# The opening of a two-layer encoder trunk in another order: gate sums split from their rows, weight splits cut in two, second tokens turned between products

## The chip, the cores and the metric

One core of one Trainium2 chip runs the whole program. The metric is the device time of one execution in microseconds (us). Each time below is either a median over runs or comes from one execution that the hardware profiler recorded.

## The reference, cut to what matters

The program computes a trunk of two layers over 1024 tokens of width 1024. What the change touches is the very first part of layer 0: the modulation of the first norm, that norm, and the first columns of the input projection.

```python
cond = jax.nn.silu(c)
for l in range(DEPTH):
    mod = cond @ w_mod[l] + b_mod[l]
    sh_a, sc_a, gt_a, sh_f, sc_f, gt_f = [m[:, None, :] for m in split_cols(mod, (D,) * 6)]
    h = rms_norm(x, g_attn[l]) * (1 + sc_a) + sh_a
    proj = h @ w_in[l]
    ...                      # three head groups, output projection, SwiGLU, residuals
return rms_norm(x, g_final)
```

Everything is fp32. A product of two fp32 matrices is made of three matmuls on operands that are split into a high part and a low rest (high by high, low by high, high by low).

## The kernel before, in words

**Engines and order.** In the opening the instruction streams of TensorE (PE), ScalarE (ACT), VectorE (DVE) and the load queue (SP) are pinned: each engine runs its instructions in the order in which the source issues them. GpSimd (POOL) is not pinned there. SP is a queue too: a load that must wait for a buffer, or for one of eight load semaphores that go round, holds up all loads behind it. So the text of the source between `wc_stage` and the end of the opening is the schedule, and nothing else decides it.

**What the opening computes.** The first 2048 columns of `w_mod` (shift and scale of the first norm) are needed before any token can be normed. They are cut into four *pairs* p = 0..3; a pair gives shift and scale for two of the eight blocks of 128 channels. Each pair is loaded in two halves, i = 2p and 2p+1, of 1 MB each (`gm_load(i)`, two transfers of 512 KB, a ring of three buffers). A half holds four groups of 128 rows. Three of them are multiplied by the condition and added up on DVE (`mod_add`, tile `ga`), the fourth is a one-row matmul on PE (`ps_mod<-gm`, called a *row* here). When both halves are in, a second matmul adds the DVE sum to the row (`ps_mod<-ga`, the *sum*), ACT copies it out (`gr`), PE turns it into columns (`ps_m`, the *turn*), and DVE makes `mod` and `gsc` of it (`gemv_finish`).

**Norm and products.** `h_blocks(half, rows, ns)` norms two blocks for 512 tokens: on DVE `nt` twice, on ACT `hh` twice (high part), on DVE `hl` twice (low part). `c_first(n)` then multiplies block n of the first 512 tokens with the weights of the third head group, into four banks: 12 matmuls. These weights come in four loads (`wc_stage`), each split into `whi` (ACT) and `wlo` (DVE) by `w_split`.

**The second tokens.** x is loaded token by token (`xn`), squared on ACT (`x_square`), turned by PE with a copy by ACT (`x_turn`, tile `xt`; `ps_x`), and its row factors are spread over the partitions by PE (`spread`, `ps_r`). For tokens 512 to 1023 this happens at the end of the opening, then `h_blocks(1, ...)` norms all eight blocks, and the projection of these tokens (`c_proj(4, 5)`, 48 matmuls, still `ps_c`) follows. `turn_vecs(1, v1)` is a small transpose for layer 1 (`pst`), with a DVE copy (`vecs`). `c_norm_first` norms the keys and queries of the first 128 tokens and hands them to POOL for the rotation.

**Behind the opening** comes a loop over t = 0..9 in which DVE and POOL norm and rotate one token block after another, PE projects and turns (`pq`, `pk`), and two more weight blocks (`wab`) are split. The first of these splits is the first `wlo` on DVE behind the opening.

**Loads.** Also in the opening: `gains_load` fetches two small vectors broadcast to 128 partitions (`g<-in_gq_ax_dram`, `g<-in_gk_ax_dram`) and four tables (`cst`), then `t5` and `mB`; `spill` writes xt to DRAM (`xd`); `sinkc` is a 6 KB load with one small DVE operation, which is issued after the pins are off, so the scheduler may place it anywhere on DVE.

Of the kernel before, what the change touches and what calls it, by code (L numbers as in the profile page):

```python
# [19 lines left out]
P = 128  # L20
# [65 lines left out]
def trunk(ctx: ExitStack, tc, A, C, out):  # L86
# [60 lines left out]
    def parts(t, a):  # L147
        return t if a == 1 else t.rearrange("p (a b) -> p a b", a=a)

    def split_tile(st, a=1, hl=None, eng=None, scale=None):  # L150
        pl, tag, bufs = hl or (wp, "whl", 8)
        hi = pl.tile([P, 1024], F32R, name="whi", tag=tag, bufs=bufs)
        lo = pl.tile([P, 1024], F32R, name="wlo", tag=tag, bufs=bufs)
        if scale is None:
            act.copy(hi, st)
            (eng or pool).tensor_tensor(out=lo, in0=st, in1=f32(hi), op=ALU.subtract)
        else:
            act.activation(hi, st, AF.Copy, scale=scale)
# [446 lines left out]
    def gm_load(i):  # L605
        gm = gms[i] = stp.tile([P, 4, 2, 2 * P], F32, name="gm", tag="gm", bufs=3)
        r0 = i % 2 * 4 * P
        for g in range(2):
            c0 = g * 1024 + i // 2 * 2 * P
            rows = A["w_mod"][0, r0 : r0 + 4 * P, c0 : c0 + 2 * P]  # L610
            sp.dma_start(gm[:, :, g, :], rows.rearrange("(k p) n -> p k n", p=P))

    def gemv_half(i):
        p, s = i // 2, i % 2
        gm = gms.pop(i).rearrange("p k g n -> p k (g n)")
        if s == 0:
            gas[p] = stp.tile([P, 4 * P], F32, name="ga", tag="ga", bufs=2)
            gps[p] = psl.tile([P, 4 * P], F32, name="ps_mod", tag="mm")
        ga, row = gas[p], gps[p][0:1]
        for k in range(3):  # L620
            mod_add(4 * s + k, ga, gm[:, k])
        pe.matmul(row, condT[:, 4 * s + 3 : 4 * s + 4], gm[:, 3], start=(s == 0), stop=False)
        if s:
            pe.matmul(row, ones, ga, start=False, stop=True)
            gas[p] = stp.tile([1, 4 * P], F32, name="gr", tag="gr", bufs=1)
            act.copy(gas[p], row)
# [54 lines left out]

    def spill(half, ns=range(KC)):
        c = slice(half * H, (half + 1) * H)
        for n in ns:
            sp.dma_start(xd[:, n, c], xt[:, n, c])

    def w_ab(l, oc):
        st = stage()
        c0 = oc * P if oc < 4 else 768 + (oc - 4) * P
        sp.dma_start(  # L690
            parts(st, KC), A["w_in"][l, :, c0 : c0 + P].rearrange("(k p) n -> p k n", p=P)
        )
        return st
# [12 lines left out]
    gm_load(1)  # L706
    wc_stage(0)
    gm_load(2)
    rxs = [stp2.tile([P, 4], F32, name="rx", tag="rx", bufs=2) for _ in range(2)]
    act.activation(c8, c8, AF.Silu)  # L710
    idle = psl.tile([P, 4, P], F32, name="ps_idle", tag="mm")

    def keep_busy(n):

        for _ in range(n):
            pe.matmul(idle, identr, bc(identr[:, None, :], [P, 4, P]), start=True, stop=True)
# [10 lines left out]
    rb = stp2.tile([P, H], F32, name="rb")  # L727
    act.copy(rb, ps)
    turn_vecs(0, v0)
    def w_split():  # L730
        wC.append(split_tile(wcs.pop(0), 2, eng=dve))

    def pair_done(p):
        gemv_turn(p)
        gemv_finish(p)
        if p == 0:
            keep_busy(8)
        h_blocks(0, rb, (2 * p, 2 * p + 1))

    gemv_half(0)  # L740
    gm_load(3)
    wc_stage(1)
    keep_busy(4)
    gemv_half(1)
    gm_load(4)
    xns[1].append(x_load(1, 0))
    w_split()
    wc_stage(2)
    keep_busy(2)
# [29 lines left out]
    x_square(1, 1, xns[1][1], rxs[1])  # L779
    c_first(4)  # L780
    c_first(5)
    w_split()
    wab.append(w_ab(0, 1))
    spill(0)
    gemv_half(7)
    pair_done(3)
# [12 lines left out]

# [1487 lines left out]
```

## Time and profile before

| | us |
|---|---|
| median of 3 runs (2466.91 to 2469.07) | 2467.94 |
| the profiled execution | 2463.24 |
| its span from first to last instruction | 2461.5 |
| start to the first transposes of x being out (0 to 14.7) | 14.7 |
| the four pairs and the eight products of the first tokens (14.7 to 69.4) | 54.7 |
| norm of the second tokens until the first product of them (69.4 to 74.1) | 4.7 |
| t loop until its last weights (74.1 to 135) | 60.9 |
| all the rest, attention, FFN and layer 1 | 2326 |

Times in the trace count from the start of the span. A row of a timeline reads: start, duration (from first to last end, if several are merged), engine, line, operation, out<-in, sizes, count; in square brackets the idle time of that engine just before, and who released it. All operations have line 49, the helper that records them, so tiles' names tell them apart. Matmuls overlap: their rows show 0.39 us each, but they start every 0.23 us. A row of a table of windows reads: stretch, its length, then busy time and count for PE, PEld (weight loads), DVE, ACT and POOL, the granted TensorE clock, the DMA share and GB/s.

### The profile page before, as it was taken

How to read it: one execution, taken by the hardware profiler on the slowest of the kernel's cores; microseconds unless marked ns; L12 is line 12 of the kernel's file. 1: busy time of each engine (PE TensorE's matmuls, PEld its weight loads, DVE VectorE, ACT ScalarE, POOL GpSimd, SP SyncE). 2: the span in 40 equal slices, each digit the busy share in tenths (PEclk: the TensorE clock that was granted, in tenths of full speed). 3: DMA queues.
4: the chain of work that ended last, by engine and by line, in shares of the span. 5: the costliest groups of instructions: out<-in, count | busy, mean ns of one | idle time of the engine just before them, and what ended most of it. 6: DMA issues, size and time to landing. Idle time of an engine off the chain costs nothing.

```text
span 2461.5 us, 33717 instructions
## 1 busy us (share of the span) xinstructions
PE 2386.7 (97%) x11733; PEld 1962.0 (80%) x11733; DVE 1789.8 (73%) x2950; ACT 1204.2 (49%) x2290; POOL 754.3 (31%) x741
## 2 busy tenths in 40 slices
PE   8999999999999999999999999999999999999998
PEld 5777898778787787888788879987877888888886
DVE  5756899976957887586677579998687545447865
ACT  3421888954543333344443148887454333334443
POOL 1520445610344343300036124464005434430001
PEclk9999999999999999999999999999999999999999
DMA  8479016054245454596434851241534322329743
GB/s 287 138 228 291 25 27 162 26 188 137 87 142 174 154 185 145 172 268 192 140 92 123 284 164 27 58 127 55 198 94 147 127 99 95 99 100 291 209 136 107
DMA packets 305338, 356.98 MB, mean 145 GB/s; under 512 B 51964, under 2 KB 221788, under 8 KB 305168
## 3 DMA queue, kind: packets, MB, share of 16 engines
q1 hardware_dynamic: 283296, 342.07, 44.7%
q10 hardware_dynamic: 21504, 12.59, 1.9%
q8 instruction: 93, 1.52, 0.3%
q14 instruction: 77, 0.63, 0.1%
q0 software_dynamic: 368, 0.17, 0.0%
HBM read 269.79 MB, written 88.63 MB: 146 GB/s over the span
## 4 chain that ended last, share of the span: by engine, by line
PE 48%; DVE 5%; issue 4%; DMA 4%; ACT 2%; POOL 1%; SPq 0%; ACTq 0%; POOLq 0%; DVEq 0%
PE ps_w L49 20%; PE ps_d L49 14%; PE ps_o L49 4%; PE pv L49 2%; PE T L49 2%; PE ps_v L49 2%; PE sC L49 2%; DMA qkd<-qko 1%; PE ps_ab L49 1%; DMA wmt<-in_w_mod_dram 1%; DMA graw<-gpd 1%; ACT pr L49 1%; PE ps_c L49 1%; DVE acc L49 1%; DVE ws L49 1%
## 5 line engine op out<-in xcount | busy, mean ns | idle before, releaser
L49 PE MATMUL ps_d<-wpt 128*128 128x512 f32 x1848 | 426.0, 391 | 3.5 <-ACT wpt L49 3.2
L49 PEld LDWEIGHTS ps_d<-wpt 128*128 128x128 f32 x1848 | 346.6, 188 | 78.2 <-issue 3.0
L49 POOL TENSOR_SCALAR pr<-pr,rs 128x384 f32<-128x384 f32 (+2 forms) x256 | 198.7, 779 | 226.1 <-DVE rs L49 211.6
L49 POOL TENSOR_TENSOR sg<-sg,u 128x512 f32<-128x512 f32 x86 | 123.6, 1439 | 379.2 <-ACT sg L49 126.9
L49 PE MATMUL pv<-pt,vs 128*128 128x256 f32 x1088 | 181.4, 296 | 13.3 <-DVE y L49 7.8
L49 ACT CAST wpt<-w 128x512 fp32r<-128x512 f32 x154 | 95.5, 620 | 194.2 <-PE ps_d L49 175.3
L49 DVE TENSOR_TENSOR pt<-T,pt 128x512 fp32r<-128x512 f32 x272 | 178.2, 680 | 4.2 <-ACT pt L49 2.4
L49 PE MATMUL T<-identr,pr 128*128 128x128 f32 x1208 | 177.4, 274 | 3.3 <-POOL pr L49 1.3
L49 ACT COPY u<-ps_w 128x512 f32<-128x512 f32 x128 | 75.1, 587 | 201.4 <-PE ps_w L49 201.4
L49 DVE TENSOR_TENSOR wpt<-w,wpt 128x512 fp32r<-128x512 f32 x154 | 108.8, 706 | 85.6 <-ACT wpt L49 83.5
L49 POOL TENSOR_TENSOR wpt<-ws,wpt 128x512 fp32r<-128x512 f32 x80 | 111.7, 1397 | 186.3 <-ACT wpt L49 137.3
L49 ACT CAST pt<-T 128x512 fp32r<-128x512 f32 x272 | 152.7, 587 | 32.1 <-PE T L49 30.0
L49 PEld LDWEIGHTS pv<-pt,vs 128*128 128x128 f32 x1088 | 144.8, 189 | 29.5 <-DVE y L49 14.3
L49 PEld LDWEIGHTS T<-identr,pr 128*128 128x128 f32 x1208 | 142.1, 141 | 22.6 <-POOL pr L49 3.6
L49 DVE SCALAR_TENSOR_TENSOR acc<-wmt,condT,acc 128x512 f32<-128x512 f32 (+1 forms) x98 | 117.2, 1207 | 50.2 <-DMA wmt<-in_w_mod_dram 49.7
L49 ACT CAST wpt<-ws 128x512 fp32r<-128x512 f32 x176 | 107.7, 622 | 64.5 <-issue 27.5
L49 DVE TENSOR_TENSOR wpt<-ws,wpt 128x512 fp32r<-128x512 f32 x96 | 86.1, 907 | 64.6 <-ACT wpt L49 64.5
L49 DVE TENSOR_REDUCE rs<-sC 128x1 f32<-128x1024 f32 x96 | 116.9, 1220 | 10.1 <-PE sC L49 10.0
L49 DVE TENSOR_TENSOR wpt<-graw,wpt 128x512 fp32r<-128x512 f32 x154 | 109.8, 713 | 18.5 <-ACT wpt L49 18.4
L49 DVE TENSOR_TENSOR ws<-wr 128x512 f32<-128x512 f32 x88 | 81.1, 924 | 50.4 <-POOL wpt L49 47.2
L49 PE MATMUL ps_w<-h22h,wpt 128*128 128x512 f32 x352 | 112.8, 402 | 4.3 <-ACT sg L49 3.6
L49 PE MATMUL sC<-qk 128*128 128x512 f32 x384 | 108.3, 404 | 6.7 <-ACT pr L49 5.1
(289 smaller groups left out, 5994.4 us busy)
## 6 DMA issues: line engine op xcount, KB each, us to landing
wr<-in_w_gu_dram SPq DMA_DIRECT2D x92, 512.0 KB, 4.1
gpd<-sg SPq DMA_DIRECT2D x154, 256.0 KB, 4.5
graw<-gpd SPq DMA_DIRECT2D x76, 512.0 KB, 3.9
w<-in_w_down_dram SPq DMA_DIRECT2D x110, 256.0 KB, 5.3
wmt<-in_w_mod_dram SPq DMA_DIRECT2D x48, 512.0 KB, 6.2
qk<-qkd SPq DMA_DIRECT2D x44, 512.0 KB, 6.7
wst<-in_w_o_dram SPq DMA_DIRECT2D x32, 512.0 KB, 4.3
wmt<-in_w_mod_dram SPq DMA_DIRECT2D x64, 256.0 KB, 3.8
```

Source lines behind the costliest of these rows:

```text
L49: ins = op(*args, **kwargs)
```

## The change

Only the opening's source is changed. `gemv_half` is cut into three parts that can stand at different places (`gemv_adds` for the DVE sums of a half, or of some of its groups; `gemv_row`; `gemv_sum`), `w_split` into `w_hi` (ACT) and `w_lo` (DVE), and the calls are put in another order.

```diff
-    def gemv_half(i):
+    def gemv_adds(i, ks=range(3)):
...
+    def gemv_row(i):
...
+    def gemv_sum(p):
+        row = gps[p][0:1]
+        pe.matmul(row, ones, gas[p], start=False, stop=True)
+        gas[p] = stp.tile([1, 4 * P], F32, name="gr", tag="gr", bufs=1)
+        act.copy(gas[p], row)
...
     gm_load(2)
+    wc_stage(1)
...
-    gemv_half(0)
+    gemv_adds(0)
+    gemv_row(0)
     gm_load(3)
-    wc_stage(1)
     keep_busy(4)
-    gemv_half(1)
+    w_hi()
+    gemv_adds(1)
+    gemv_row(1)
+    gemv_sum(0)
+    w_lo()
     gm_load(4)
-    xns[1].append(x_load(1, 0))
-    w_split()
+    for j in range(2):
+        xns[1].append(x_load(1, j))
     wc_stage(2)
-    keep_busy(2)
-    pair_done(0)
+    for j in range(2, 4):
+        xns[1].append(x_load(1, j))
+    gemv_turn(0)
+    gemv_row(2)
+    keep_busy(4)
+    pair_h(0)
     pssC = [psl.tile([P, 512], F32, name="ps_c", tag="mm") for _ in range(T0)]
-    gemv_half(2)
+    w_hi()
+    gemv_adds(2)
+    c_first(0)
+    gemv_row(3)
     gm_load(5)
-    xns[1].append(x_load(1, 1))
-    c_first(0)
-    w_split()
+    gemv_adds(3)
+    w_lo()
+    c_first(1)
+    gemv_sum(1)
     wc_stage(3)
-    c_first(1)
-    gemv_half(3)
     gm_load(6)
-    xns[1].append(x_load(1, 2))
-    gemv_half(4)
-    gm_load(7)
-    xns[1].append(x_load(1, 3))
-    pair_done(1)
-    x_square(1, 0, xns[1][0], rxs[1])
+    gemv_adds(4, (0,))
+    gemv_turn(1)
+    gemv_row(4)
+    pair_h(1)
+    w_hi()
+    for j in range(2):
+        x_square(1, j, xns[1][j], rxs[1])
+    gemv_adds(4, (1, 2))
     c_first(2)
-    c_first(3)
-    w_split()
-    wab = [w_ab(0, 0)]
+    gemv_row(5)
+    gemv_adds(5)
+    w_lo()
     g8 = gains_load(ccp, 0)
...
     sp.dma_start(mB, C["maskB"])
-    gemv_half(5)
-    gemv_half(6)
-    pair_done(2)
...
+    gm_load(7)
+    c_first(3)
+    gemv_sum(2)
+    wab = [w_ab(0, 0)]
+    gemv_adds(6, (0,))
+    gemv_turn(2)
+    gemv_row(6)
+    x_turn(1, xns[1], range(2), (act, act))
+    pair_h(2)
+    w_hi()
     for j in (2, 3):
         x_square(1, j, xns[1][j], rxs[1])
+    gemv_adds(6, (1, 2))
+    c_first(4)
+    gemv_row(7)
+    gemv_adds(7)
+    w_lo()
+    spill(0)
+    wab.append(w_ab(0, 1))
+    x_turn(1, xns[1], range(2, 4), (act, act))
     x_rms(rxs[1])
-    x_turn(1, xns[1], range(4), (act, act))
+    c_first(5)
+    gemv_sum(3)
+    gemv_turn(3)
+    rows = spread(rxs[1], 0, psl)
+    x_turn(1, xns[1], range(4, 6), (act, act))
+    pair_h(3)
+    x_turn(1, xns[1], range(6, KC), (act, act))
     c_first(6)
-    x_turn(1, xns[1], range(4, KC), (act, act))
     c_first(7)
+    turn_vecs(1, v1)
+    for n in range(0, KC, 2):
+        h_blocks(1, rows, (n, n + 1))
     spill(1)
-    rows = spread(rxs[1], 0, psl)
-    turn_vecs(1, v1)
...
     first_t1 = c_norm_first(pssC[0], gm[:, 0:512], gm[:, 512:1024], gm[:, 1024:1032])
...
-    for n in range(0, KC, 2):
-        h_blocks(1, rows, (n, n + 1))
```

The matmuls that only keep PE busy go from 4 + 2 + 8 to 4 + 4 between the first row and the first product. Behind the opening every engine's stream is the same as before, apart from two small things: the DVE operation on `sinkc` stands earlier, and one table write (`skA`) stands later in the SP queue.

Three places on which the prediction rests, with names as the program numbers them (`wst`, `gm`, `xn`: load buffers; `gr`: a pair's sums; `nt`, `hh`, `hl`: the norm).

First, SP around the last half of `w_mod`, now:

```order
L49 DMA gm_348<-in_w_mod_dram 128x4x256 [waits DMAHW1_49,PE_49]
L49 DMA gm_348<-in_w_mod_dram 128x4x256 [waits DMAHW2_49]
L49 DMA g8_394<-in_gq_ax_dram 128x6x64 [waits DMAHW3_49]
L49 DMA g8_394<-in_gk_ax_dram 128x2x64 [waits DMAHW4_49]
L49 DMA cst_398<-const_rope_dram 128x128 [waits DMAHW5_49]
L49 DMA t5_406<-in_t5_table_dram 32x6 [waits DMAHW1_49]
L49 DMA mB_408<-const_maskB_dram 6x512 [waits DMAHW2_49]
L49 DMA gm_410<-in_w_mod_dram 128x4x256 [waits DMAHW3_49,DVE_49,PE_49]
L49 DMA gm_410<-in_w_mod_dram 128x4x256 [waits DMAHW4_49]
```

`gm_348` is the seventh half (i = 6), `gm_410` the eighth (i = 7). Before, the eighth half stood ahead of the two broadcast loads `g8`; now it stands behind them, and its two transfers wait for the load semaphores (3 and 4) that the two broadcast loads use.

Second, ACT around pair 2, before and now:

```order
L49 COPY gr_433<-ps_mod_356 1x512 [waits PE_49,Activation_49]
L49 ACTIVATE hh_107<-nt_448,mod0_82 128x512 [waits DVE_49]
L49 ACTIVATE hh_107<-nt_450,mod0_82 128x512 [waits DVE_49]
L49 ACTIVATE xt_103,rx_152<-xn_311 128x2x512 [waits DMAHW5_49,Activation_49]
L49 CAST whi_481<-wst_329 128x1024 [waits DMAHW6_49]
```

```order
L49 COPY gr_426<-ps_mod_358 1x512 [waits PE_49]
L49 COPY xt_103<-ps_x_439 128x512 [waits PE_49]
L49 COPY xt_103<-ps_x_445 128x512 [waits PE_49]
L49 ACTIVATE hh_107<-nt_453,mod0_82 128x512 [waits DVE_49]
L49 ACTIVATE hh_107<-nt_455,mod0_82 128x512 [waits DVE_49]
```

Two copies of turned second tokens now stand between the pair's sums and its norm. Pair 3 has two such copies at the same place.

Third, DVE from the last pair to the second tokens, before and now:

```order
L49 COPY vecs1_81<-pst_606 128x72 [waits PE_49]
L49 TENSOR_REDUCE gm_609<-gm_609 128x8 [waits Activation_49]
L49 RECIPROCAL gm_609<-gm_609 128x8 [waits Activation_49]
L49 TENSOR_TENSOR gm_609<-ps_c_298,gm_609 128x512 [waits DVE_49]
L49 TENSOR_TENSOR gm_609<-gm_609,g8_412 128x512 [waits DMAHW7_49,DVE_49,Pool_49]
L49 SCALAR_TENSOR_TENSOR nt_627<-xt_103,gsc0_84,ps_r_601 128x512
```

```order
L49 SCALAR_TENSOR_TENSOR hl_108<-nt_550,mod0_82,hh_107 128x512 [waits Activation_49]
L49 COPY vecs1_81<-pst_592 128x72 [waits PE_49]
L49 SCALAR_TENSOR_TENSOR nt_595<-xt_103,gsc0_84,ps_r_529 128x512
L49 SCALAR_TENSOR_TENSOR nt_597<-xt_103,gsc0_84,ps_r_529 128x512 [waits DVE_49]
L49 SCALAR_TENSOR_TENSOR hl_108<-nt_595,mod0_82,hh_107 128x512 [waits Activation_49]
L49 TENSOR_SCALAR sinkc_86<-sinkc_86 128x12 [waits DMAHW0_49]
L49 SCALAR_TENSOR_TENSOR hl_108<-nt_597,mod0_82,hh_107 128x512 [waits Activation_49]
```

The four operations of `c_norm_first` have gone from ahead of the second tokens' norm to behind it; the copy of `pst`, which PE makes only behind the eighth product, still stands ahead of the norm; and the operation on `sinkc` stands between the first two low parts.

More of the change, by code (lines that the diff above doesn't have):

```diff
@@ L611, in gm_load @@
             sp.dma_start(gm[:, :, g, :], rows.rearrange("(k p) n -> p k n", p=P))
-    def gemv_half(i):
+    def gemv_adds(i, ks=range(3)):
         p, s = i // 2, i % 2
-        gm = gms.pop(i).rearrange("p k g n -> p k (g n)")
+        if i % 2 == 0 and 0 in ks:
+            gas[p] = stp.tile([P, 4 * P], F32, name="ga", tag="ga", bufs=2)
+        for k in ks:
+            mod_add(4 * s + k, gas[p], gms[i][:, k].rearrange("p g n -> p (g n)"))
+    def gemv_row(i):
+        p, s = i // 2, i % 2
         if s == 0:
-            gas[p] = stp.tile([P, 4 * P], F32, name="ga", tag="ga", bufs=2)
             gps[p] = psl.tile([P, 4 * P], F32, name="ps_mod", tag="mm")
[L619 to L626, printed above, removed]
+        k = 4 * s + 3
+        pe.matmul(
+            gps[p][0:1], condT[:, k : k + 1], gms[i][:, 3].rearrange("p g n -> p (g n)"),
+            start=(s == 0), stop=False,
+        )
+    def gemv_sum(p):
[3 more added lines that the diff above has]
+        act.copy(gas[p], row)
     def gemv_turn(p):
@@ L729, in trunk, with w_hi, w_lo, pair_h @@
     turn_vecs(0, v0)
[L730 to L734, printed above, removed]
+    whs = []
+    def w_hi():
+        st = wcs.pop(0)
+        hi, lo = (
+            wp.tile([P, 1024], F32R, name=f"w{p}", tag="whl", bufs=8) for p in ("hi", "lo")
+        )
+        act.copy(hi, st)
+        whs.append((st, hi, lo))
+        wC.append((parts(hi, 2), parts(lo, 2)))
+    def w_lo():
+        st, hi, lo = whs.pop(0)
+        sub(lo, st, f32(hi))
+    def pair_h(p):
         gemv_finish(p)
-        if p == 0:
-            keep_busy(8)
         h_blocks(0, rb, (2 * p, 2 * p + 1))
-    gemv_half(0)
+    gemv_adds(0)
+    gemv_row(0)
     gm_load(3)
-    wc_stage(1)
     keep_busy(4)
-    gemv_half(1)
+    w_hi()
[3 more added lines that the diff above has]
+    w_lo()
     gm_load(4)
-    xns[1].append(x_load(1, 0))
-    w_split()
+    for j in range(2):
+        xns[1].append(x_load(1, j))
     wc_stage(2)
-    keep_busy(2)
-    pair_done(0)
+    for j in range(2, 4):
[4 more added lines that the diff above has]
+    pair_h(0)
     pssC = [psl.tile([P, 512], F32, name="ps_c", tag="mm") for _ in range(T0)]
-    gemv_half(2)
+    w_hi()
+    gemv_adds(2)
+    c_first(0)
+    gemv_row(3)
     gm_load(5)
-    xns[1].append(x_load(1, 1))
-    c_first(0)
-    w_split()
+    gemv_adds(3)
+    w_lo()
+    c_first(1)
+    gemv_sum(1)
     wc_stage(3)
-    c_first(1)
-    gemv_half(3)
     gm_load(6)
-    xns[1].append(x_load(1, 2))
-    gemv_half(4)
-    gm_load(7)
-    xns[1].append(x_load(1, 3))
-    pair_done(1)
-    x_square(1, 0, xns[1][0], rxs[1])
+    gemv_adds(4, (0,))
[6 more added lines that the diff above has]
+    gemv_adds(4, (1, 2))
     c_first(2)
-    c_first(3)
-    w_split()
-    wab = [w_ab(0, 0)]
+    gemv_row(5)
+    gemv_adds(5)
+    w_lo()
     g8 = gains_load(ccp, 0)
@@ L775, in trunk @@
     sp.dma_start(mB, C["maskB"])
-    gemv_half(5)
-    gemv_half(6)
-    pair_done(2)
[L779 to L786, printed above, removed]
+    gm_load(7)
[8 more added lines that the diff above has]
+    w_hi()
     for j in (2, 3):
         x_square(1, j, xns[1][j], rxs[1])
-    x_rms(rxs[1])
-    x_turn(1, xns[1], range(4), (act, act))
+    gemv_adds(6, (1, 2))
[6 more added lines that the diff above has]
+    x_turn(1, xns[1], range(2, 4), (act, act))
+    x_rms(rxs[1])
+    c_first(5)
[5 more added lines that the diff above has]
+    x_turn(1, xns[1], range(6, KC), (act, act))
     c_first(6)
-    x_turn(1, xns[1], range(4, KC), (act, act))
     c_first(7)
+    turn_vecs(1, v1)
+    for n in range(0, KC, 2):
+        h_blocks(1, rows, (n, n + 1))
     spill(1)
-    rows = spread(rxs[1], 0, psl)
-    turn_vecs(1, v1)
     gm = stp.tile([P, 2048], F32, name="gm", tag="gm", bufs=3)
```

## The prediction

> **What bounds the kernel now.** I read the table of windows over the whole span first. All the change touches lies before 75 us, and what follows is full:
>
> ```profile
> 14.70:69.40 54.70, 45.70 (x185) 27.71 (x185) 33.99 (x54) 20.56 (x34) 3.77 (x5) 0.97 0.84 283
> 74.10:135.00 60.90, 59.11 (x278) 46.92 (x278) 50.89 (x77) 27.35 (x57) 35.71 (x30) 0.96 0.46 124
> 135.00:2461.00 2326.00, 2269.74 (x11212) 1878.02 (x11212) 1697.79 (x2804) 1145.01 (x2180) 707.80 (x691) 1.00 0.46 141
> ```
>
> PE has 2270 of 2326 us of work behind 135, in an order that does not change. So the change is worth what the opening hands over earlier, no more. Inside the opening I read the PE timeline; these rows show a pair between two groups of products, the end, and the first product of the second tokens:
>
> ```profile
> 24.90 0.49 PE L49 MATMUL ps_c<-whi,hh 128*128 128x512 f32 x1 [0.61 <-ACT hh L49]
> 31.24 1.02 PE L49 MATMUL ps_mod<-gm,condT 128*1 128x512 f32 x2
> 32.09 1.02 PE L49 MATMUL ps_mod<-ga,onesr 128*1 128x512 f32 x2
> 36.30 0.50 PE L49 MATMUL ps_c<-whi,hh 128*128 128x512 f32 x1 [1.99 <-ACT hh L49]
> 37.09 0.50 PE L49 MATMUL ps_c<-whi,hl 128*128 128x512 f32 x1 [0.29 <-DVE hl L49]
> 43.49 1.02 PE L49 MATMUL ps_mod<-ga,onesr 128*1 128x512 f32 x2
> 47.69 0.49 PE L49 MATMUL ps_c<-whi,hh 128*128 128x512 f32 x1 [1.99 <-ACT hh L49]
> 56.44 1.02 PE L49 MATMUL ps_mod<-ga,onesr 128*1 128x512 f32 x2
> 60.58 0.49 PE L49 MATMUL ps_c<-whi,hh 128*128 128x512 f32 x1
> 64.26 2.12 PE L49 MATMUL ps_x<-identr,xn 128*128 128x128 f32 x16
> 69.44 0.23 PE L49 MATMUL pst<-identr,v 72*128 72x72 f32 x1
> 74.07 0.80 PE L49 MATMUL ps_c<-whi,hh 128*128 128x512 f32 x1 [4.41 <-ACT hh L49]
> ```
>
> From a pair's sum to its first product is 36.30 - 32.09 = 4.2 us, and 4.2 again for 43.49 to 47.69: a chain PE, ACT `gr`, PE turn, DVE `mod` and `nt`, ACT `hh`, PE. It is serial in the new order too. A row takes PE 0.85 (31.24 to 32.09). The two products of a pair take 0.8 to the first low part and 23 more starts until the next row, which stands 0.85 ahead of 43.49: (42.64 - 37.09) / 23 = 0.24 each, 6.3 together.
>
> What comes after the first product of the second tokens is not bound by PE but by DVE:
>
> ```profile
> 69.70 0.23 DVE L49 COPY vecs<-pst 128x72 f32<-128x72 f32 x1 [5.75 <-PE pst L49]
> 72.52 1.40 DVE L49 SCALAR_TENSOR_TENSOR nt<-xt,gsc,ps_r 128x512 f32<-128x512 f32 x2
> 85.15 1.23 DVE L49 TENSOR_TENSOR wlo<-wst,whi 128x1024 fp32r<-128x1024 f32 x1
> 88.40 0.39 PE L49 MATMUL ps_ab<-hh,wlo 128*128 128x512 f32 x1
> 107.70 3.28 POOL L49 TENSOR_TENSOR ct<-cq,cst 128x512 f32<-128x512 f32 x3 [1.70 <-issue]
> 112.32 2.85 POOL L49 TENSOR_TENSOR wlo<-wst,whi 128x1024 fp32r<-128x1024 f32 x1
> 115.23 0.50 PE L49 MATMUL ps_ab<-hh,wlo 128*128 128x512 f32 x1 [0.32 <-POOL wlo L49]
> ```
>
> DVE runs without a wait worth the name from the copy of `pst` at 69.70 through the norm of the second tokens to the weight split that ends at 86.3. PE needs that split at 88.40, 2.1 later; POOL, fed by DVE, makes the next one, and for that PE waits 0.32 at 115.23. So the moment at which PE makes `pst` (call it T, now 69.44) starts the chain that ends last for the next 45 us, and the gain is 69.44 minus the new T, not what PE alone saves.
>
> **The change part by part.** All sums are against the profiled execution (2463.24, its span 2461.5); the difference is then put on the median of 2467.94.
>
> *Pair 0.* The split stands differently:
>
> ```profile
> 20.25 0.58 ACT L49 COPY gr<-ps_mod 1x512 f32<-1x512 f32 x1 [5.76 <-PE ps_mod L49]
> 20.74 1.04 ACT L49 CAST whi<-wst 128x1024 fp32r<-128x1024 f32 x1
> 21.81 1.23 DVE L49 TENSOR_TENSOR wlo<-wst,whi 128x1024 fp32r<-128x1024 f32 x1 [2.67 <-ACT whi L49]
> 22.95 0.15 DVE L49 TENSOR_TENSOR mod<-ps_m,vecs 128x4 f32<-128x4 f32 x1
> 33.21 0.58 ACT L49 COPY gr<-ps_mod 1x512 f32<-1x512 f32 x1 [6.75 <-PE ps_mod L49]
> 29.32 2.32 DVE L49 SCALAR_TENSOR_TENSOR ga<-gm,condT,ga 128x512 f32<-128x512 f32 x3
> ```
>
> `mod` came only when `wlo` was done. `whi` now stands ahead of `gr`, so `wlo` runs as soon as DVE's sums end, about 19.1, and is out of the way at 20.3. `gr` stays at 20.25, and the product follows `gr` by 36.30 - 33.21 = 3.1, as in pair 1: 23.3 instead of 24.90, **1.6 gained**. The row of half 2 and four idle matmuls fit in front of it.
>
> *Pair 1.* First low part 24.1, eleven more starts 2.6, row 3 0.85, second product 2.85: sum at 30.4; 4.2 later, 34.6, the first product, against 36.30: **1.7 ahead**. The rows were moved from the gaps to between products, which costs PE the same 0.85 there; DVE's sums (2.3 for a half's three) follow the pair's norm from 24.6 and end for both halves near 29, before the sum needs them.
>
> *Pair 2.* Half 5 is now the 22nd and 23rd load of 512 KB instead of the 19th and 20th, because the four loads of second tokens stand ahead. Before, the 29 loads to the first of `wab` end near 47; at 345 GB/s a load takes 1.52:
>
> ```profile
> 20.00:30.00 10.00, 9.09 (x37) 5.82 (x37) 7.92 (x12) 3.85 (x5) 0.00 (x0) 1.00 1.01 345
> 47.00:53.00 6.00, 5.01 (x14) 3.77 (x15) 4.61 (x6) 3.28 (x5) 0.00 (x0) 0.72 0.12 32
> ```
>
> So the 23rd lands near 47 - 6 x 1.52 + 0.4 = 38.3, and row 5 waits 0.35 for it. Sum at 42.05 (43.49 before). But then ACT copies two blocks of second tokens ahead of `hh`. Eight such copies take 3.98, 0.5 each:
>
> ```profile
> 63.64 3.98 ACT L49 COPY xt<-ps_x 128x512 f32<-128x512 f32 x8
> ```
>
> Their transposes come behind row 6, so `hh` starts 1.2 later than the chain alone would have it: product at 47.4 instead of 47.69. **Nearly all of the 1.7 is spent: 0.3 ahead.**
>
> *The clock.* Behind 47.69 the products ran at half the clock for one stretch, and the second tokens' products for two:
>
> ```profile
> 45.20:48.60 3.40, 1.12 (x7) 0.63 (x7) 2.66 (x6) 1.68 (x3) 0.00 (x0) 1.00 0.54 139
> 48.60:52.10 3.50, 3.50 (x9) 2.73 (x10) 2.28 (x3) 1.68 (x3) 0.00 (x0) 0.51 0.11 30
> 72.60:79.40 6.80, 4.94 (x11) 3.52 (x12) 6.53 (x10) 2.76 (x4) 4.71 (x4) 0.50 0.42 140
> ```
>
> Nine starts in 3.5 instead of 15: 1.4 to 1.7 lost in the first, about 2.5 in the second (11 starts in 6.8, less the two waits); ahead of the first lies a stretch of 3.4 with PE busy for 1.1. The same wait at 36.30 brought none, so it also hangs on where the gap falls. In the new order row 6 and two turns fill that gap; the thin place is now pair 1 (sum to product, one row inside). I take the first stretch as gone, and half a chance of another of 1.6: 0.8 as a cost. The Trainium skill, "TensorE: Matmul & The Clock Gate", Part 1, has the clock halved after at least one idle window of about 3.4 us, windows that run free of the kernel; the trace agrees, with 3.5 us at 0.51. By that rule the sum below would be 2.2 with no such window and 0.6 with one.
>
> *Row 7 and the last half.* The fifth product group ends at 47.4 + 0.8 + 11 x 0.24 = 50.8, then row 7 needs half 7. Its two transfers now wait until the two broadcast loads have landed. What those take:
>
> ```profile
> g<-in_gq_ax_dram SPq DMA_DIRECT2D x1, 192.0 KB, 14.3
> 54.97 0.40 SPq L49 DMA_DIRECT2D wst<-in_w_in_dram  x1
> 1189.10 13.26 DMA g<-in_gq_ax_dram
> DMA to landing us min/median/max: 4.1/7.0/11.1
> ```
>
> 192 KB take 14.3 us from issue to landing, and 13.3 in layer 1, where little was queued ahead; a load of SP waited for it till 54.97. In the new order it is issued when the load eight before, the 19th, has landed, 47 - 10 x 1.52 + 0.4 = 32.2, and lands at 45.6 to 46.6. Half 7 is then issued, and lands 4.1 (the least for such a load) to 5 later: 50.5 to 52. I take 51.1, a wait of **0.3**. Behind row 7 come two turns (1.0) and product 5 (2.85): sum of pair 3 at 51.1 + 0.9 + 1.0 + 2.85 = 55.9, 0.5 ahead of before, where the half clock had slowed the same products.
>
> *Pair 3 and the end.* `hh` again stands behind two copies, which wait for the spread: first product 5.1 behind the sum, at 60.9 (60.58). Then the two products run through, without the four turns (2.12) and the spread (0.45) that stood there: T = 60.9 + 6.3 = 67.2. **Gain 69.44 - 67.2 = 2.2.**
>
> *Behind T.* PE's first product of the second tokens comes 2.0 behind T (0.4 to `nt`, then 74.07 - 72.52) instead of 4.6, since `c_norm_first` no longer stands ahead. But DVE has the same work from T to the weight split, so PE's lead (2.6 here, 2.5 in clock) turns into a wait at the first `ps_ab`, of about 2.5. Worth nothing. The small operation on `sinkc` stands among the norms now and not later. I put both at 0.
>
> *`sinkc`.* It waits for its load, which SP issues behind eight stores of xt:
>
> ```profile
> 64.23 11.54 SPq L49 DMA_DIRECT2D xd<-xt  x8
> sinkc<-in_sink_sw_dram SPq DMA_DIRECT2D x1, 6.0 KB, 4.2
> ```
>
> The last copy of a turned block is at 62.2, the load goes out at 63.5 and lands 4.2 later, 67.7; DVE comes to it at T + 2.7 = 69.9. No wait, with 2 to spare.
>
> Sum: 2.2 - 0.8 = 1.4; 2467.94 - 1.4 = **2466.5**.
>
> **The rivals.**
>
> *PE's gain in full.* If the DVE chain has more slack than its rows show, PE alone sets the end: its first product of second tokens at 69.2, against 74.07 plus 2.5 of half clock: 7.4 gained, 2460.5. For it: the table gives DVE only 51 of 61 us there. Against: POOL's split at 115.23 already holds PE up, and DVE's next 16 us behind 69.70 show no idle time worth the name.
>
> *Half 7 late (slower).* If the broadcast loads only begin when the 26 loads ahead have drained (42.4), they land at 42.4 + 13.3 = 55.7. Half 7, behind them and the four tables, comes at 61, row 7 waits 10, T = 61 + 16.1 = 77.1: 7.7 lost, and 1.6 of half clock behind so long a gap: 2477. From a landing at 53.3 on it costs, from 58 on more than 0.2%. For it: in 47 to 53 only 32 GB/s moved, with the tables queued behind. Against: queues of 6 and of 3 us ahead gave 14.3 and 13.3, so the time runs mostly beside the queue. In between, 8 behind the drain (47 to 54.97 before): T 72, 2470.5. The Trainium skill, "DMA: Bandwidth & Descriptors", section "Queues, rings and completion order", has each DMA engine take the transfers of one queue in order; that speaks for tables and half 7 standing behind, as the 32 GB/s do.
>
> *`sinkc` holds DVE.* If the stores take as long as before (64.23 to 75.77 on SP), the load lands 2 later than DVE wants it; T's gain is eaten: 2468. It changes no sign.
>
> **How the numbers follow.** 0.2% (4.9 us) is about what a measurement of this kernel can tell from no change. The forecast, with the wait on `sinkc` and the middle case of half 7, stays inside that: 0.57. PE's gain in full: 0.25, all of it faster. Half 7 late beyond 58: 0.18, slower. The likeliest alone reaches from 2463.5 to 2470.5. For 8 in 10 I go up to the first rival's 2460.5 and down to 2472.5, a landing of half 7 near 57.
>
> **What would show it.** Right: the first product near 23.3, product group 4 near 47.4, row 7 without a long wait, `pst` near 67, PE waiting over 2 us at the first `ps_ab` for DVE's `wlo`, and 115.23's wait moved by T's shift alone. Wrong: a gap of several us ahead of row 7 with the broadcast loads landing behind 50; `hl` waiting on `sinkc`; half clock over the products of pairs 1 to 3; or a first `ps_ab` without a wait, which would leave PE its whole gain.

## The result, and the profile after

| kernel | median us | range us, executions | to the kernel before |
|---|---|---|---|
| before | 2467.78 | 2462.56 to 2471.68, 12 | 1 |
| changed | 2469.68 | 2467.28 to 2473.80, 12 | 1.0014 (1.0004 to 1.0025) |
| forecast | 2466.5 | 2460.5 to 2472.5 | 0.9994 |

The changed kernel is a little slower, by 0.14%, not a little faster by 0.06%. The time lies inside the range, on the other side of no change; the miss is 3.2 us. The profiled execution of the changed kernel took 2473.80 (its span 2472.0), 10.6 more than that of before, and is the slowest of its twelve. The comparison goes by the medians: behind 135 us both run the same order, and single executions of the kernel before lie up to 9 us apart.

First PE's timeline in the changed kernel, the rows that answer to those shown of before (start, duration, operation; in brackets the wait ahead of it and what ended it):

```profile
21.46 1.86 PE L49 MATMUL ps_mod<-gm,condT 128*1 128x512 f32 x2
25.13 0.63 PE L49 MATMUL ps_c<-whi,hh 128*128 128x512 f32 x1
33.09 1.02 PE L49 MATMUL ps_mod<-ga,onesr 128*1 128x512 f32 x2
37.23 0.50 PE L49 MATMUL ps_c<-whi,hh 128*128 128x512 f32 x1 [1.04 <-ACT hh L49]
46.18 1.02 PE L49 MATMUL ps_mod<-ga,onesr 128*1 128x512 f32 x2
51.59 0.49 PE L49 MATMUL ps_c<-whi,hh 128*128 128x512 f32 x1 [1.34 <-ACT hh L49]
55.40 1.02 PE L49 MATMUL ps_mod<-gm,condT 128*1 128x512 f32 x2 [0.20 <-DMA gm<-in_w_mod_dram]
60.17 1.02 PE L49 MATMUL ps_mod<-ga,onesr 128*1 128x512 f32 x2
65.06 0.49 PE L49 MATMUL ps_c<-whi,hh 128*128 128x512 f32 x1 [0.45 <-ACT hh L49]
71.30 0.23 PE L49 MATMUL pst<-identr,v 72*128 72x72 f32 x1
88.56 0.50 PE L49 MATMUL ps_ab<-hh,wlo 128*128 128x512 f32 x1 [2.82 <-DVE wlo L49]
117.36 0.50 PE L49 MATMUL ps_ab<-hh,wlo 128*128 128x512 f32 x1 [0.58 <-POOL wlo L49]
```

`pst` stands at 71.30, 1.86 later than before's 69.44; forecast was 67.2. The last row is the one that waited for POOL at 115.23 before: 2.13 later, about as much, so in this trace what happens at `pst` is handed on.

Two things in these rows were not in the sum. The first product is late (25.13, not 23.3), and row 7, at 55.40, is late although it waited only 0.20. The windows give the first; columns are busy time (and count) of PE, its weight loads, DVE, ACT and POOL, then the granted clock, the DMA share and GB/s:

```profile
17.00:20.90 3.90, 1.02 (x2) 0.09 (x2) 3.27 (x4) 1.62 (x2) 0.00 (x0) 0.99 1.08 362
20.90:27.60 6.70, 6.65 (x16) 4.05 (x17) 5.73 (x10) 2.32 (x3) 0.00 (x0) 0.50 1.09 358
37.20:41.50 4.30, 3.98 (x10) 2.95 (x11) 4.18 (x6) 3.78 (x6) 0.00 (x0) 0.60 0.85 270
41.00:50.00 9.00, 8.34 (x35) 4.30 (x34) 4.56 (x8) 0.74 (x3) 0.09 (x1) 0.98 0.19 53
```

From 20.9 to 27.6 PE ran at half its clock, and again through part of pair 1. The last of these rows belongs to the second thing: for 9 us the DMA engines moved 53 GB/s, after 358 in the second row. What stood in SP's queue:

```profile
34.45 1.60 SPq L49 DMA_DIRECT2D g<-in_gq_ax_dram  x1
49.90 0.96 SPq L49 DMA_DIRECT2D gm<-in_w_mod_dram  x2
DMA to landing us min/median/max: 14.0/14.7/15.4
SPq L49 <- DMA g<-in_gq_ax_dram: 6.4, 1, 6.4
```

The third row is that of the two broadcast loads `g` (from the view of this tile), the fourth SP's wait ahead of half 7. The first load was issued at 34.45 and landed 15.4 later, at 49.85; only then did SP issue half 7, and row 7 ran 5.5 behind that. Which of the two, the lost clock or the late half 7, makes the changed kernel slower, this one trace cannot tell, since in it both end at the same moment, 55.2 to 55.4. The experiments start there.

### The profile page after: what moved, and what is told of

It is laid out like the page before. It is cut to its first block, busy times and chain, and to the rows that moved or that the text cites. A ratio compares the mean times of both kernels' runs of the same rounds, so it can differ in the third digit from the quotient of the medians.

```text
span 2472.0 us, 33704 instructions
## 1 busy us (share of the span) xinstructions
PE 2397.8 (97%) x11727; PEld 1965.7 (80%) x11727; DVE 1790.1 (72%) x2950; ACT 1202.1 (49%) x2290; POOL 756.5 (31%) x741
## 4 chain that ended last, share of the span: by engine, by line
PE 50%; DVE 7%; issue 4%; DMA 3%; ACT 2%; POOL 2%; SPq 0%; POOLq 0%; ACTq 0%; DVEq 0%
PE ps_w L49 21%; PE ps_d L49 12%; PE ps_o L49 4%; PE ps_ab L49 3%; PE pv L49 2%; PE T L49 2%; PE ps_v L49 2%; PE sC L49 2%; DMA wmt<-in_w_mod_dram 1%; DVE wpt L49 1%; DVE acc L49 1%; DVE ws L49 1%; DMA w<-in_w_down_dram 1%; ACT pr L49 1%; PE ps_c L49 1%
## 5 line engine op out<-in xcount | busy, mean ns | idle before, releaser
L49 PE MATMUL pv<-pt,vs 128*128 128x256 f32 x1088 | 181.9, 296 | 13.3 <-DVE y L49 7.8
L49 ACT CAST wpt<-ws 128x512 fp32r<-128x512 f32 x176 | 107.7, 622 | 66.7 <-issue 27.6
L49 ACT CAST wpt<-graw 128x512 fp32r<-128x512 f32 x154 | 95.1, 617 | 58.2 <-DMA graw<-gpd 49.8
```

The lines of the kernel that those rows point to most:

```text
L49: ins = op(*args, **kwargs)
```

## The experiments

Twelve kernels, in order; all are the changed kernel with the edit shown (cut short where `...` stands) but for one, which is the kernel before with an edit. Each ratio is to runs of the kernel before on the same chip.

**Two idle matmuls put back.**

```diff
     gemv_sum(0)
 ...
+    keep_busy(2)
     gemv_turn(0)
```

> Changed kernel with two idle matmuls put back between the sum of pair 0 and its turn. Theory (clock): in the changed kernel PE is busy for 1.02 of 17.0 to 20.9 us and runs at 0.50 of the clock from 20.9 to 27.6; with the gap filled this stretch goes, row 2 takes 1.0 again, the first product starts near 23.5 instead of 25.13 and the sum of pair 1 stands near 30.5 instead of 33.09. But half 7 still lands near 55.2, so row 7 waits about 2 for it instead of 0.20, pst stays near 71, and the time stays within 1.5 us of the changed kernel's 2469.7. Rival (order alone): the first product is late because row 2 and four idle matmuls stand ahead of it; it starts at 24.9 or later, at whatever clock, and nothing else moves. Second rival: SP's loads are paced by PE, half 7 moves with the rows, and pst comes near 69: 2467.5.

Measured: 2471.45, ratio 1.0017 (1.0005 to 1.0030). The stretch stayed:

```profile
20.90:27.60 6.70, 6.70 (x18) 3.91 (x18) 5.57 (x10) 2.32 (x3) 0.00 (x0) 0.54 1.09 360
25.29 0.63 PE L49 MATMUL ps_c<-whi,hh 128*128 128x512 f32 x1
55.61 1.02 PE L49 MATMUL ps_mod<-gm,condT 128*1 128x512 f32 x2 [0.75 <-DMA gm<-in_w_mod_dram]
```

The first half of the theory falls: with the idle matmuls back the half clock is still there (0.54). Its second half, that row 7 stands at half 7's landing all the same, holds (the time is 1.8 above the changed kernel's, a little outside the 1.5 named).

**Half 7 ahead of the broadcast loads.**

```diff
     gemv_adds(4, (1, 2))
+    gm_load(7)
     c_first(2)
 ...
     sp.dma_start(mB, C["maskB"])
-    gm_load(7)
     c_first(3)
```

> Changed kernel with the two loads of half 7 issued ahead of the broadcast loads and tables, as soon as half 4's buffer is free. Theory (PE's own lateness sets row 7 in the changed kernel, half 7's landing near 55.2 coinciding with it): half 7 lands before 48, row 7 has no wait, and pst moves by no more than 0.3 from 71.30; time unchanged within 1 us of 2469.7. Rival (half 7 is what made the change slower, the slower rival of the prediction): pst comes 2 or more earlier, 2467.5 or less. If g arrives too late for the norm of the first tokens, DVE waits for it behind 83.

Measured: 2466.97, ratio 1.0002 (0.9992 to 1.0012).

```profile
23.26 0.50 PE L49 MATMUL ps_c<-whi,hh 128*128 128x512 f32 x1
52.83 1.02 PE L49 MATMUL ps_mod<-gm,condT 128*1 128x512 f32 x2
68.73 0.23 PE L49 MATMUL pst<-identr,v 72*128 72x72 f32 x1
```

Row 7 has no wait and `pst` comes 2.6 sooner: the rival holds. But this execution also had the full clock at its start, with PE's order there as in the changed kernel. So the half clock of 20.9 to 27.6 comes in some executions and not in others, and one trace with it says little; and the first run's rival, that the order alone makes the first product late, falls with the 23.26.

**Both edits.**

```diff
+    keep_busy(2)
     gemv_turn(0)
 ...
     gemv_adds(4, (1, 2))
+    gm_load(7)
     c_first(2)
 ...
-    gm_load(7)
     c_first(3)
```

> Both edits: two idle matmuls before the turn of pair 0, and half 7's loads ahead of the broadcast loads. If the lost clock of the start and the landing of half 7 are two bounds that cover each other, each edit alone gives at most 0.5 at pst, and both together 2 to 2.5: pst near 69, time near 2467.3. If the clock alone is it, this is as the first of the two; if neither, pst stays at 71.3.

Measured: 2465.56, ratio 0.9994 (0.9983 to 1.0004). This execution had no half clock from 14.7 to 69.4 (granted clock 1.00), and so shows what the new order is by itself:

```profile
23.25 0.50 PE L49 MATMUL ps_c<-whi,hh 128*128 128x512 f32 x1
34.84 0.50 PE L49 MATMUL ps_c<-whi,hh 128*128 128x512 f32 x1 [1.04 <-ACT hh L49]
47.71 0.49 PE L49 MATMUL ps_c<-whi,hh 128*128 128x512 f32 x1 [1.34 <-ACT hh L49]
51.25 1.02 PE L49 MATMUL ps_mod<-gm,condT 128*1 128x512 f32 x2
56.02 1.02 PE L49 MATMUL ps_mod<-ga,onesr 128*1 128x512 f32 x2
60.91 0.49 PE L49 MATMUL ps_c<-whi,hh 128*128 128x512 f32 x1 [0.45 <-ACT hh L49]
67.14 0.23 PE L49 MATMUL pst<-identr,v 72*128 72x72 f32 x1
84.31 0.50 PE L49 MATMUL ps_ab<-hh,wlo 128*128 128x512 f32 x1 [2.81 <-DVE wlo L49]
113.11 0.50 PE L49 MATMUL ps_ab<-hh,wlo 128*128 128x512 f32 x1 [0.50 <-POOL wlo L49]
```

Row 7 at 51.25 instead of 55.40 is 4.15; `pst` at 67.14 instead of 71.30 is 4.16. What half 7's lateness costs at row 7 arrives at `pst` in full, and the two stretches of half clock ahead of it in the changed kernel's trace cost nothing on top: they were covered by the wait for half 7.

**`pst` ahead of the last two products of the first tokens.**

```diff
     x_turn(1, xns[1], range(6, KC), (act, act))
+    turn_vecs(1, v1)
     c_first(6)
     c_first(7)
-    turn_vecs(1, v1)
```

> Changed kernel with pst and its copy ahead of the last two products of the first tokens. Nothing that the norm of the second tokens reads comes from pst; DVE only meets its copy first. Theory (the prediction's claim: the DVE chain behind pst ends last for the next 40 us): the copy comes near 66.4 instead of 71.56, the norm of the second tokens 5 earlier, PE has no wait of 1.73 at their first product and less than 0.5 instead of 2.82 at the first ps_ab, and without that wait no half clock behind 88.5 (1.7): 107 us of before's count comes 4 to 6 earlier than in the changed kernel, time 2463.5 to 2465.5. Rival (POOL or csq is the bound there): PE starts the second tokens earlier but meets a like wait at the first or second ps_ab weights; gain under 2, 2468 or more. Second rival: the norm of the first tokens on ACT and DVE comes late, and its rope on POOL ends later than before.

Measured: 2463.57, ratio 0.9986 (0.9973 to 0.9998), with half 7 as late as ever:

```profile
55.23 1.74 PE L49 MATMUL ps_mod<-gm,condT 128*1 128x512 f32 x2 [3.06 <-DMA gm<-in_w_mod_dram]
67.84 0.22 DVE L49 COPY vecs<-pst 128x72 f32<-128x72 f32 x1
84.78 0.51 PE L49 MATMUL ps_ab<-hh,wlo 128*128 128x512 f32 x1 [0.47 <-DVE wlo L49]
88.50:92.50 4.00, 3.53 (x23) 2.87 (x22) 3.16 (x6) 1.01 (x3) 3.92 (x4) 1.00 0.02 6
```

The first row is the clearest of the late half 7: PE, with less half clock behind it, now waits 3.06 for it and still runs row 7 at 55.23. DVE's copy comes 3.7 sooner, not the expected 5.2: row 7 stands where it stood, but behind its wait the clock was 0.72 (56 to 61) and the sum of pair 3 came 1.5 later than in the changed kernel (61.63, 60.17), and the copy now follows the low parts of that pair. The first `ps_ab` with a low part comes 3.8 sooner, and no half clock follows. The DVE chain is what ends last, as the prediction said; its start at `pst` was only a matter of order.

**Half 7 and `pst` early.** The edits of the second and the fourth run.

```diff
     gemv_adds(4, (1, 2))
+    gm_load(7)
 ...
+    turn_vecs(1, v1)
     c_first(6)
```

> Changed kernel with half 7's loads ahead of the broadcast loads and with pst ahead of the last two products of the first tokens. Theory: two separate bounds, which add. Without the late half 7, row 7 stands near 51 to 53 instead of 55.23, so hl of pair 3, behind which the norm of the second tokens now starts, comes 2.5 to 5 earlier than in the run with pst early alone (67.3), and so does the first ps_ab with a low part (84.78 there): 80 to 82.5, time 2459 to 2461.5 against 2463.6. Rival: with pst early, the chain of the first norm (csq, rope on POOL, its gains landing near 54) or the low weights for ps_ab bind, and nothing is added: 2463 or more.

Measured: 2458.50, ratio 0.9973 (0.9959 to 0.9987), the first `ps_ab` with a low part at 82.35, although 20.9 to 27.6 and 37.2 to 41.5 had a clock of 0.57 and 0.64. The two add, a little beyond the forecast.

**Half 7 early, ACT's copies behind `hh`.**

```diff
+    gm_load(7)
     c_first(2)
 ...
-    x_turn(1, xns[1], range(2), (act, act))
     pair_h(2)
+    x_turn(1, xns[1], range(2), (act, act))
 ...
-    x_turn(1, xns[1], range(4, 6), (act, act))
     pair_h(3)
+    x_turn(1, xns[1], range(4, 6), (act, act))
```

> Changed kernel with half 7's loads early and with ACT's copies of turned second tokens behind hh instead of ahead of it, in pairs 2 and 3. Theory (the copies delay hh, 1.07 for two of them by the changed kernel's rows): the wait ahead of product group 4 falls from 1.34 to about 0.3 and that ahead of group 6 from 0.45 to 0.1 or less, pst comes 1.2 to 1.5 earlier than with half 7 early alone, clock aside (67.14 without a half clock): 65.7 to 66, time near 2465.7. Rival: the turned blocks' accumulators come free later, and the next transposes or products wait for the copies; no gain, 2467.

Measured: 2462.75, ratio 0.9995 (0.9981 to 1.0009). Both waits for `hh` that the copies had made, 1.34 and 0.45, are gone, but the last turns now wait for an accumulator that ACT has not yet emptied:

```profile
60.83 0.66 PE L49 MATMUL ps_x<-identr,xn 128*128 128x128 f32 x4 [1.24 <-ACT xt L49]
66.91 0.23 PE L49 MATMUL pst<-identr,v 72*128 72x72 f32 x1
```

`pst` is at 66.91, with a clock of 0.75 in 20.9 to 27.6. The intervals of this run and of half 7 alone overlap, so what the copies are worth in time is not settled.

**Half 7 directly behind `g`.**

```diff
-        for _ in range(4):
-            rope_load(pl)
+        if l:
+            for _ in range(4):
+                rope_load(pl)
 ...
     g8 = gains_load(ccp, 0)
+    gm_load(7)
+    for _ in range(4):
+        rope_load(ccp)
     t5 = ccp.tile([32, 6], F32, name="t5")
 ...
-    gm_load(7)
     c_first(3)
```

> Changed kernel with the two loads of half 7 directly behind the two broadcast loads g, and the four cst loads, t5 and mB behind them; the first 26 loads and g as in the changed kernel. It tells SP's wait from the order of the transfers. Theory (SP holds the issue until the load eight before has landed; in the changed kernel that is g's first): half 7 now waits only for earlier loads, is issued near 39 instead of 49.90, and lands before 46, ahead of g; row 7 has no wait, time near 2467. Rival (transfers of one queue land in order, so half 7 is behind the broadcast loads however early it is issued): it lands at 49.5 or later, and row 7 comes between 51 and 56.

Measured: 2469.53, ratio 1.0017 (1.0005 to 1.0030).

```profile
38.58 9.66 SPq L49 DMA_DIRECT2D gm<-in_w_mod_dram  x2
56.08 1.44 PE L49 MATMUL ps_mod<-gm,condT 128*1 128x512 f32 x2 [3.58 <-DMA gm<-in_w_mod_dram]
DMA to landing us min/median/max: 3.3/14.9/16.6
```

(The last row is that of tile `gm` from 30 to 60.) SP begins to issue half 7 11 sooner than in the changed kernel, and it lands no sooner. Of the four loads in the last row the least took 3.3; the two of half 7 took 15.9 and 16.6. The issue of the second held SP until 48.24 (38.58 + 9.66), but the first was issued in 0.8 and landed only near 54.5, so half 7 is late without any wait of SP's. The theory falls, the rival holds in what it says of the landing.

**All four edits.**

```diff
+    keep_busy(2)
 ...
+    gm_load(7)
 ...
+    x_turn(1, xns[1], range(2), (act, act))
 ...
+    turn_vecs(1, v1)
```

> Changed kernel with all four edits: two idle matmuls back, half 7 early, copies behind hh, pst ahead of the last two products. If the late half 7, the copies and the order of DVE behind pst are separate bounds: first ps_ab with a low part 1.2 to 1.5 earlier than with half 7 and pst early, time 2457.5 to 2460, faster than both kernels by 0.3%. The idle matmuls are worth nothing by the first runs (the half clock came with them at 20.9 and stayed away without them). Rival: DVE's own work behind hl of pair 3 or POOL's rope binds, so the copies add nothing: 2460 to 2462.

Measured: 2458.96, ratio 0.9970 (0.9956 to 0.9984). That is 0.3% below the kernel before, inside the theory's 2457.5 to 2460 and outside the rival's 2460 to 2462; its first `ps_ab` with a low part stands at 80.47, 1.9 sooner than with half 7 and `pst` early (82.35). But the time is level with that of those two edits alone (2458.50, 0.9973), so what the copies are worth stays open here too.

**`g` on ACT's queue.**

```diff
-        sp.dma_start(g8[:, 0:6, :], bc(A["gq_ax"][l][None, None, :], [P, 6, 64]))
-        sp.dma_start(g8[:, 6:8, :], bc(A["gk_ax"][l][None, None, :], [P, 2, 64]))
+        (sp if l else act).dma_start(g8[:, 0:6, :], bc(A["gq_ax"][l][None, None, :], [P, 6, 64]))
+        (sp if l else act).dma_start(g8[:, 6:8, :], bc(A["gk_ax"][l][None, None, :], [P, 2, 64]))
```

> Changed kernel with the two broadcast loads g issued by ACT, at the same place of the program, so that they leave SP's queue; half 7 stays behind the cst loads, t5 and mB. Theory (in the changed kernel half 7 is late because it stands behind g in one queue, as the run with half 7 directly behind g showed, landing near 55.9 although issued near 39): half 7 now lands before 47, row 7 has no wait, pst comes near 67.1 to 68.7, time near 2467 as with half 7 early. Rival (the broadcast loads keep the DMA engines themselves busy, whatever the queue): half 7 lands at 50 or later, row 7 waits 1 or more, 2469 to 2471.

Measured: 2470.65, ratio 1.0022 (1.0012 to 1.0032).

```profile
DMA to landing us min/median/max: 11.9/11.9/11.9
50.93 0.28 SPq L49 DMA_DIRECT2D mB<-const_maskB_dram  x1
51.32 0.95 SPq L49 DMA_DIRECT2D gm<-in_w_mod_dram  x2
```

(The first row is that of tile `g`.) `g` is issued at 39.0 on ACT's queue and lands at 50.9. SP waits 9.5 for just that ahead of mB, and issues half 7 only behind it: the load semaphores go round the loads of both queues, and mB's is one that `g` has taken. The rival's numbers came (row 7 at 56.79 with a wait of 3.96), but half 7 was held at its issue once more, so this run says nothing of how the transfers share the DMA engines. The next run is without that hold.

**The same with half 7, `pst` and the copies.**

```diff
+        (sp if l else act).dma_start(g8[:, 0:6, :], bc(A["gq_ax"][l][None, None, :], [P, 6, 64]))
 ...
+    gm_load(7)
     c_first(2)
 ...
+    x_turn(1, xns[1], range(2), (act, act))
 ...
+    turn_vecs(1, v1)
     c_first(6)
```

> Changed kernel with half 7 early, pst ahead of the last two products, copies behind hh, and the broadcast loads on ACT's queue. Beside the run of all four edits this has nothing behind the broadcast loads any more (w_ab's weights, the stores of xt). Theory: those are needed late enough, the chain from the sum of pair 3 over DVE sets the end: as all four edits, 2457.5 to 2460. Rival: the weights for ps_ab or the gains come sooner and spare a wait behind 80: 2457 or less.

Measured: 2466.27, ratio 0.9998 (0.9989 to 1.0007): neither theory. Half 7 was late again:

```profile
31.71 9.32 SPq L49 DMA_DIRECT2D gm<-in_w_mod_dram  x4
56.61 1.02 PE L49 MATMUL ps_mod<-gm,condT 128*1 128x512 f32 x2 [2.77 <-DMA gm<-in_w_mod_dram]
41.00:45.00 4.00, 4.00 (x15) 2.28 (x15) 2.92 (x4) 0.00 (x0) 0.52 (x1) 0.97 0.08 24
```

Both loads of half 7 are issued by 41.03, on a queue that `g` is not in, but row 7 gets the second only at 56.6, while the 16 DMA engines move 24 GB/s over 41 to 45. With `g` on SP's queue behind half 7 that had cost nothing; with `g` on ACT's queue it is issued at 39.8, beside half 7, and holds it up. So standing in the same queue is not what it takes. The Trainium skill, "DMA: Bandwidth & Descriptors", section "Issuing engines are not separate DMA queues", says that loads issued by different engines run on the same 16 DMA engines and interleave. The rows fit shared engines, and a landing 15.9 behind the issue shows how little the interleaving helped here. Behind row 7 this trace runs level with that of `pst` early alone (first low part of `ps_ab` at 84.67 and 84.78), whose ratio of 0.9986 (0.9973 to 0.9998) overlaps; so half 7, late once more, took back what its early issue had given.

**The kernel before, with half 7 late.**

```diff
-    gm_load(7)
     xns[1].append(x_load(1, 3))
 ...
-    wab = [w_ab(0, 0)]
     g8 = gains_load(ccp, 0)
 ...
     sp.dma_start(mB, C["maskB"])
+    gm_load(7)
+    wab = [w_ab(0, 0)]
```

> The kernel before, with one thing of the change: half 7's loads moved behind the broadcast loads, the cst loads, t5 and mB. Theory (this move alone costs what the change loses): half 7 lands near 57, its three sums on DVE and the sum of pair 3 follow, near 60 instead of 56.44, pst 3 later than 69.44, and the time goes up by 2.5 to 4: ratio 1.001 to 1.0016. Rival (the loss lies elsewhere in the change, in the order of pair 0 and 1 or ACT's copies): pst within 1 of 69.44, ratio within 0.0005 of 1.

Measured: 2470.06, ratio 1.0015 (1.0007 to 1.0024), as much as the whole change loses. The first of `wab`'s loads moves behind half 7 too, as in the change.

```profile
59.05 1.02 PE L49 MATMUL ps_mod<-gm,condT 128*1 128x512 f32 x2 [2.38 <-DMA gm<-in_w_mod_dram]
61.39 1.86 PE L49 MATMUL ps_mod<-ga,onesr 128*1 128x512 f32 x2 [1.32 <-DVE ga L49]
76.87 0.23 PE L49 MATMUL pst<-identr,v 72*128 72x72 f32 x1
```

PE waits 2.38 for half 7 and 1.32 more for DVE's sums of it; `pst` is later by 7.4, more than the 3 expected, since the products behind that wait ran at half the clock (0.50 in 61 to 65). The median is only 3.8 above before's; how much of the 7.4 is the move and how much the clock of this one execution, the trace does not tell.

**`g` from other addresses.** The gains are left out of the first layer here; the loads have as many pieces of the same size.

```diff
+            gx = A["x"][0, 0:P, :].rearrange("p (h d) -> p h d", d=128)[:, :, 0:64]
+            sp.dma_start(g8[:, 0:6, :], gx[:, 0:6, :])
+            sp.dma_start(g8[:, 6:8, :], gx[:, 6:8, :])
```

> Changed kernel, order untouched; the first layer's gains tile g is filled from 128 rows of x (pieces of 64 numbers, each from an address of its own) instead of the one row of gains repeated 128 x 8 times. As many pieces of 256 B on the same queue at the same place; the gains are left out of the first layer. Theory (the loads are slow, and hold up what stands behind them on every queue, since all pieces read one address): g lands within 6 us of issue instead of 15.4, half 7 is issued before 42 and lands before 47, row 7 has no wait, pst comes near 67.2 to 69, time near 2467. Rival (many small pieces are slow as such): g takes 13 to 15 again, row 7 waits or stands at 55, 2469.7.

Measured: 2465.21, ratio 0.9992 (0.9983 to 1.0002), with the order of the changed kernel untouched.

```profile
33.99 4.35 SPq L49 DMA_DIRECT2D g<-in_x_dram  x2
DMA to landing us min/median/max: 7.5/8.3/9.1
43.18 1.38 SPq L49 DMA_DIRECT2D gm<-in_w_mod_dram  x2
41.00:50.00 9.00, 6.70 (x30) 3.59 (x29) 4.72 (x9) 3.60 (x6) 2.23 (x3) 1.00 0.75 192
52.27 1.02 PE L49 MATMUL ps_mod<-gm,condT 128*1 128x512 f32 x2
68.15 0.23 PE L49 MATMUL pst<-identr,v 72*128 72x72 f32 x1
```

`g` lands in 7.5 to 9.1 instead of 14.0 to 15.4 (the expected 6 left out that its pieces start only when the queue ahead has drained, near 40.5), half 7 is issued at 43.18 instead of 49.90, and row 7 has no wait. The pieces have the same number and size and differ only in where they read, so that is what makes the load slow, and not that its pieces are many and small. The repeated address is the likely reason; that the other addresses lie far apart, and in another tensor, was not told apart from it.

## Why the prediction was wrong

**The step that failed** is the one on row 7: "Half 7 is then issued, and lands 4.1 (the least for such a load) to 5 later: 50.5 to 52. I take 51.1, a wait of 0.3." The half landed near 55.2. Of the 4.1 us between, the issue of `g` gave 2.25 (34.45, not 32.2), its time to landing 1.1 (15.4, not 14.3), and half 7 itself the rest. The reasoning under it was that the time of `g` "runs mostly beside the queue", from 14.3 and 13.3 with different queues ahead. In the changed kernel the queue ahead drained near 41, and `g` needed 8.9 more: the case between that the prediction named, "8 behind the drain (47 to 54.97 before): T 72, 2470.5". It came as T 71.30 and 2469.68. So the path was seen and one term of it mis-sized: the end of `g`, counted from its issue instead of from the end of the queue ahead (42.4 + 8 = 50.4 by the prediction's own rows, 49.85 measured). Why `g` in the second layer took 13.3 with little ahead is not settled.

That this one step makes the difference is shown from both sides:

| half 7 | kernels | ratio to before |
|---|---|---|
| late (row 7 at 55.4 to 59) | changed; idle matmuls back; behind `g`; `g` on ACT's queue; before with half 7 late | 1.0014, 1.0017, 1.0017, 1.0022, 1.0015 |
| in time, `pst` unmoved (row 7 at 50.9 to 52.8) | half 7 early; with idle matmuls; with copies; `g` from other addresses | 1.0002, 0.9994, 0.9995, 0.9992 |

Each interval of the first row lies above 1, and each of the second contains 1. So the loss and its cause are shown. That the forecast gain (0.9994) is there once half 7 is in time is not shown, though these ratios fit it.

**Pair 0, pair 1, pair 2, pair 3: right.** Without half clock and with half 7 in time (the run of both edits) the first products of pairs 0 to 3 stand at 23.25, 34.84, 47.71 and 60.91, where the prediction had 23.3, 34.6, 47.4 and 60.9; the sum of pair 3 at 56.02 (55.9), `pst` at 67.14 (67.2). The copies ahead of `hh` cost the wait of 1.34 that was put at 1.2.

**What T is worth: right at the place named.** At 115.23 before, the shift was 2.13 later for 1.86 at `pst`, and 2.12 sooner for 2.30. PE's lead turned into a wait of 2.82 at the first `ps_ab` (forecast 2.5). The first `ps_ab` with a low part itself stands only 0.16 later than before (88.56, 88.40), because DVE's split had ended 2.1 ahead of PE's need there. What the prediction did not see is that this wait can bring a half clock of its own behind it (0.57 in 88.5 to 92.5 in the changed kernel), and that the chain need not start at `pst`: with `pst` early the kernel is 0.14% faster than before even with half 7 late.

**The clock: too small, and covered.** Half a chance of one stretch of 1.6 was taken, in pair 1. The trace has two ahead of row 7; they cost 1.88 at the first product (25.13 to 23.25) and 3.87 by the sum of pair 2 (46.18 to 42.31). All of it went into the wait for half 7. Where half 7 is in time such a stretch does count, and for the 1.6 that was taken: with half 7 early alone the clock was 0.75 in 37.2 to 41.5, and the sum of pair 2 and `pst` came 1.6 later (43.88, 68.73) than in the run of both edits (42.31, 67.14). The Trainium skill, "TensorE: Matmul & The Clock Gate", Part 1, has the windows of the clock run free of the kernel. The traces agree, since the same order up to the first product ran at 0.50 in the changed kernel's execution and at 1.00 in that with half 7 early (20.9 to 27.6 in both).

**The rivals.** PE's gain in full did not come: the wait for DVE stands at the first `ps_ab` in every run of the new order with `pst` in its place (1.68 to 2.82). `sinkc` held nothing: DVE reached it without a wait. Half 7 late was the true one, in its middle form; its far form (a landing at 61) did not come.

## What to carry to other kernels

A load that is moved ahead of another is priced by when the other can be issued and by what the engines then still have to do, not by its own time from issue to landing; where two readings of such a time are both open, the forecast belongs to the one that a row behind it (the drained queue, 47 to 54.97) already shows. A short row that is repeated over all partitions goes behind every load that something waits for, or on its own when nothing does. And before a lost clock is blamed for a later time, look for a transfer that ends at the same moment and would have cost as much without it.

The version to keep is the changed kernel with half 7 ahead of the broadcast loads and `pst` ahead of the last two products: 2458.50, 0.9973 (0.9959 to 0.9987) of the kernel before.

## What the runs showed of the hardware that was not expected

Two loads whose 1024 pieces of 256 B (128 x 8) read the same two rows hold up transfers of another queue as well: with 1 MB of half 7 issued on SP's queue and `g` on ACT's, the DMA engines moved 24 GB/s over 41 to 45, and half 7's second load landed 15.9 behind its issue. In the changed kernel, with half 7 not yet issued, they took 14.0 to 15.4 from issue to landing, against 7.5 to 9.1 when as many pieces had addresses of their own.

The half clock can come although PE is not idle all through the stretch ahead: PE was busy for 1.02 of the 3.9 us ahead of it, its longest wait there was 2.35, and the same work was followed by the full clock in other executions. Where PE waits long (2.8 at the first `ps_ab`, 3.96 for half 7 with `g` on ACT's queue) the clock is halved behind it in several of the runs, not in all.
